# Recurrent layer of a two-layer encoder: input products by chunks through rotating PSUM banks, gates over two PSUM tiles, one exponential less, finished rows stored already split

## The chip, the cores and the metric

The kernel runs as one program on one core of a Trainium2 chip. The measured quantity is the device time of one execution in microseconds (us). The core has five engines that run their own instruction streams and wait for each other by semaphores: PE (TensorE, matrix products), DVE (VectorE), ACT (ScalarE), POOL (GpSimd) and SP (SyncE, which here issues every DMA). Matrix products land in PSUM, a memory of eight banks of 512 float32 columns by 128 partitions. Everything else lives in SBUF, or in DRAM between two stages.

## The reference, cut to what matters

The model has two layers over 1,040 tokens (16 meta tokens and 1,024 others) of width 1,024. The first is an attention layer, which the change does not touch. The second is recurrent:

```python
def odd_layer(z, w_in, conv_w, conv_b, w_a, b_a, w_x, b_x, lam, w_out):
    zp = z @ w_in                                  # (1040, 4096)
    u, gate = split_cols(zp, (2048, 2048))
    xc = conv_b + sum(pad(u)[tap:tap + T] * conv_w[tap] for tap in range(4))
    y = lru(xc, 0, reverse=False) + lru(xc, 1, reverse=True)
    return (y * silu(gate)) @ w_out

def lru(xc, d, reverse):                           # 16 blocks of 128 features
    r = sigmoid(xb @ w_a[d] + b_a[d]); i = sigmoid(xb @ w_x[d] + b_x[d])
    log_a = -8 * r * softplus(-lam[d])
    a = exp(log_a)
    b = sqrt(-expm1(2 * log_a)) * i * xc
    h_t = a_t * h_(t-1) + b_t                      # along the tokens
```

## The kernel before

**Number format.** Each matrix product is made of three products of a high and a low part, `hi` and `lo`, that are multiplied as float32r. Splitting a row means one rounding copy and one subtraction. Weights come by DMA into `wr` (256 KB each) and are split on POOL: line 106 writes `wh`, line 107 subtracts and writes `wl` (`wown` for the gates' weights). The weight rings have three `wr` and four `wh`/`wl` buffers.

**Blocks.** Features stand on the partitions, tokens along the rows. The recurrent layer goes through 16 blocks `e` of 128 features. For each block PE makes `pu`, the input product of `u` (three chunks of 348, 346 and 346 columns over eight contraction tiles, 72 matrix instructions), and `pg`, that of the gate (two chunks of 512, 48 instructions). Each is made in two halves of the contraction: in `half`, all chunks of the first four tiles stand ahead of all chunks of the other four. DVE scales `pu` into `ou` (line 1148). ACT and DVE make the convolution `oxc` (lines 1151 to 1154), which is split into `oxh` (ACT, line 757) and `oxl` (DVE, line 758). The silu of the gate is `og`, `otg` (lines 1140 to 1143).

**Two blocks behind.** While block e's input products run, PE also makes the four gate products `pz` of block e-1 (two directions, `r` and `i`), whose sigmoids are written as tanh (line 1180). For each direction ACT makes `oa` = a (line 1187), `osq` = a squared by a second exponential (line 1190) and a third tanh into `tz` (line 1191). DVE forms (osq + 1) * tz (line 1192) and (z + 1) * xc (line 1193). The rest of the recurrence belongs to block e-2 and is emitted after block e's convolution: one square root over both directions (ACT, line 1200, with a table load ahead of it and another behind it), a product (line 1203) and a scan (lines 1205 and 1207) per direction on DVE, the sum of the directions on POOL (line 1210), the product with the silu on DVE (line 1211), and a store of the finished row to DRAM (line 1212).

**Order.** A scheduler works out each engine's instruction order beforehand from the order in which the kernel emits work; weight loads and splits are emitted with a priority 200 steps ahead. On the chip each engine then takes its instructions in that order.

**PSUM.** One buffer of three banks for `pu`, a `big` tile of three banks for the gate products of both directions, and a `two` tile of two banks for `pg`.

**End.** The output product `oo` has eight tiles of 128 output features with 96 matrix instructions each, four quarters `qd` of the contraction of four finished rows each. The rows come back from DRAM in `y_load` (`oy`) and are split there: the first four while blocks 12 to 15 run (on POOL and DVE), the other twelve after block 15 (on ACT and DVE).

Of the kernel before, what the change touches and what calls it, by code (L numbers as in the profile page):

```python
# [16 lines left out]
P = 128  # L17
T = 1040
# [23 lines left out]
def trunk_kernel(ctx: ExitStack, tc: tile.TileContext, a: dict, out: bass.AP):  # L42
# [51 lines left out]
    def split_w(src, shape, nm, own=None, eng=nc.gpsimd):  # L94
# [4 lines left out]
        if own:  # L99
            hi, lo = [sb["P"].tile([P, 512], F32R, tag=own + z, name="wown", bufs=1) for z in "hl"]  # L100
# [48 lines left out]
    def parts(nm):  # L149
        """A row of T columns over three banks: (bank, first column, last column)."""  # L150
# [18 lines left out]
    def stat(sq, s, m, dst, tag=None, rt="S"):  # L169
        """Sums over features of the squares in sq, one row per selector column; the matrix part is put off."""  # L170
# [66 lines left out]
    s_y = [dram.tile([P, 1024], F32, name=f"s_y{i}") for i in range(16)]  # L237

# [188 lines left out]
    def fold(r, j, t0, t1):  # L427
        """Squares of a head's 128 features as two rows of 64, the pair's second head below the first."""
# [52 lines left out]
    def mla_scales():  # L481
        # score scales of the latent attention, by token, and the key norms, by row
# [45 lines left out]
    def steps(g, res):  # L528
        """Pass on the times that g yields; its tile goes to res."""
# [119 lines left out]
    class Unit:  # L649
        """One block of queries of two heads in the windowed attention."""  # L650
# [239 lines left out]
    def parts_c(nm, third="t"):  # L890
        """A row of T columns in the banks of the latent attention."""
# [169 lines left out]
    out_mm(ps0[0], 0, 0, 1)  # L1061
    ph.close()
    ph = phase(None, H=16, T=4, rs=1)
# [27 lines left out]
    psum({"b": 1, "big": 1, "two": 1})  # L1091

# [4 lines left out]
    # decay constants: c1 = -(8 / 2) * softplus(-lambda), half biases  # L1097
# [22 lines left out]
    c2n = const.tile([P, 32], F32, name="c2n")  # L1120
    nc.vector.tensor_scalar(c2n, pl_, -8.0, None, ALU.mult)
    c1p = const.tile([P, 32], F32, name="c1p")
    nc.vector.tensor_scalar(c1p, pl_, 4.0, None, ALU.mult)
# [4 lines left out]
    def w_gates(e):  # L1128
        return split_w(a["wg"][e], (4, P), "wg", "gw" if e < 15 else None)
# [4 lines left out]
    def half(e, isu, hf, ps):  # L1134
        wh, wl = split_w(a["w2"][2 * e + isu, hf], (4, P), "w2")
        mm3p(ps, [(wh[:, k], wl[:, k], h1h[4 * hf + k], h1l[4 * hf + k]) for k in range(4)], hf == 0, hf == 1)

    def gate_in(e, pg):
        g = row("og", "T")
        nc.vector.scalar_tensor_tensor(g[:, :1024], pg, 0.5, R["rs2"][:, NM:T], ALU.mult, ALU.mult)  # L1140
        tg = row("otg", "T")
        nc.scalar.activation(tg[:, :1024], g[:, :1024], AF.Tanh)
        nc.vector.scalar_tensor_tensor(tg[:, :1024], tg[:, :1024], 1.0, g[:, :1024], ALU.add, ALU.mult)
        return tg

    def conv(e, pu):
        u = row("ou", "X")
        evac(pu, lambda t, c: nc.vector.tensor_mul(u[:, c], t, R["rs2"][:, c]))
        xc = row("oxc", "X")
        cw = [vcol(V_CW + 4 * e + t) for t in range(4)]  # L1150
        nc.scalar.activation(xc, u, AF.Identity, scale=cw[2], bias=vcol(V_CB + e))
        nc.vector.scalar_tensor_tensor(xc[:, 2:T], u[:, 0:T - 2], cw[0], xc[:, 2:T], ALU.mult, ALU.add)
        nc.vector.scalar_tensor_tensor(xc[:, 1:T], u[:, 0:T - 1], cw[1], xc[:, 1:T], ALU.mult, ALU.add)  # L1153
        nc.vector.scalar_tensor_tensor(xc[:, 0:T - 1], u[:, 1:T], cw[3], xc[:, 0:T - 1], ALU.mult, ALU.add)
        return xc

    class Lru:
        """The recurrence of one block of features, in both directions."""

        def __init__(self, e, tg, xc, ch_, cl_):  # L1160
            self.e, self.tg, self.xc, self.c = e, tg, xc, (ch_, cl_)
            self.z = {}
# [4 lines left out]
        def gate(self, d, j, ps=None):  # L1167
            gh, gl = self.w
            e = self.e
            if ps is None:  # L1170
                ps = big("pz")
            n = T if d == 0 else T - NM
            ch, off = (CH, OFF) if d == 0 else (CHR, -NM)
# [4 lines left out]
            src = ps[:, OFF:OFF + T] if d == 0 else ps[:, :n]  # L1178
            bc = hb[:, 32 * j + 16 * d + e:32 * j + 16 * d + e + 1]
            nc.scalar.activation(z[:, :n], src, AF.Tanh, scale=0.5, bias=bc)  # L1180
            self.z[d, j] = z
# [14 lines left out]
        def scan(self):  # L1196
            tz = self.tz
            if True:
                nc.vector.memset(tz[:, 1, 1024:T], 0.0)
# [212 lines left out]
```

## Time and profile before

| what | value |
|---|---|
| median of 3 runs | 1963.94 us (1963.55 to 1967.7) |
| span of the profiled execution | 1963.5 us; no other time is shown for this execution, and the lowest of the three runs is 1963.55 us |
| granted TensorE clock, mean | 0.980 |
| busy: PE, DVE, ACT, POOL | 94%, 65%, 44%, 46% |
| recurrent layer, from its first product to the last instruction | 1241.6 to 1963.5 us |

PE, DVE, ACT and POOL are as above; PEld is PE's weight load and SPq the DMA queue of SP. In a timeline row stand the start and the duration in us, the engine, the line of the kernel, the operation and its output and input tiles, and in brackets the idle time before it and what ended it. In a row of a group the three numbers after the count are the shortest, the median and the longest duration in ns. In a row of the windows the engines' busy times in us are followed by the granted clock, the busy share of the DMA engines and the rate in GB/s. In a row of the chain stand start and length in us.

### The profile page before, as it was taken

The numbers are of one execution on the slowest core, as the hardware profiler recorded it, in microseconds if no ns is written. First come the engines' busy times: TensorE is split into PE (matmuls) and PEld (weight loads), VectorE is DVE, ScalarE is ACT, GpSimd is POOL, SyncE is SP. The second block draws the span as 40 slices with busy tenths as digits, with TensorE's granted clock in tenths as the row PEclk, the third lists the DMA queues.
The fourth block names the chain that finished last, engine by engine and source line by source line (L and its number), as shares of the span: only waits on it lengthen the run. The fifth ranks groups of instructions, "written<-read, shape, count | busy, mean of one in ns | idle before, by whom it ended". The sixth has DMA issues, their size and how long they took to land.

```text
span 1963.5 us, 28463 instructions
## 1 busy us (share of the span) xinstructions
PE 1837.2 (94%) x10822; PEld 1666.7 (85%) x10822; DVE 1272.3 (65%) x1953; ACT 859.7 (44%) x1394; POOL 908.1 (46%) x769
## 2 busy tenths in 40 slices
PE   8999989889999999998999999998989898889899
PEld 7987988889999999887888899887778787777687
DVE  7785368787663424889888743467878787887200
ACT  5355234454332202665666531156565656556000
POOL 5454455444225732434333333455656565654431
PEclk9999999999999999999999999999999998989899
DMA  5356422223223452322221023311111122124421
GB/s 177 82 171 248 116 77 69 63 69 85 81 64 128 152 174 90 87 88 67 66 75 52 23 87 131 92 53 54 59 54 60 54 68 67 65 79 147 171 81 43
DMA packets 107606, 180.19 MB, mean 92 GB/s; under 512 B 31759, under 2 KB 51343, under 8 KB 107470
## 3 DMA queue, kind: packets, MB, share of 16 engines
q1 hardware_dynamic: 107470, 178.37, 29.0%
q8 instruction: 85, 1.39, 0.3%
q14 instruction: 51, 0.42, 0.1%
HBM read 123.57 MB, written 46.77 MB: 87 GB/s over the span
## 4 chain that ended last, share of the span: by engine, by line
PE 50%; DVE 24%; ACT 8%; POOL 7%; issue 6%; DMA 3%; SPq 0%; POOLq 0%; DVEq 0%; ACTq 0%
PE pj L159 10%; PE oo L159 7%; PE pxop L159 6%; PE px L917 4%; PE av L997 4%; PE op L159 3%; PE up L159 3%; PE tp L981 3%; POOL osq L1210 3%; PE vps L425 2%; DVE osq L1207 2%; DVE oz L1203 2%; DVE oxc L1153 2%; DVE osq L1205 2%; DVE tz L1192 2%
## 5 line engine op out<-in xcount | busy, mean ns | idle before, releaser
L106 POOL TENSOR_SCALAR wh<-wr 128x512 fp32r<-128x512 f32 (+2 forms) x219 | 178.1, 813 | 522.5 <-PE pu L159 132.4
L107 POOL TENSOR_TENSOR wl<-wr,wh 128x512 fp32r<-128x512 f32 (+2 forms) x219 | 350.8, 1602 | 17.5
L159 PE MATMUL pj<-xh,wl 128*128 128x346 f32 (+1 forms) x768 | 252.0, 329 | 12.3 <-DVE wl L107 6.9
L159 PE MATMUL pj<-xl,wh 128*128 128x346 f32 (+1 forms) x768 | 249.6, 325 | 0.3 <-DVE xl L259 0.3
L159 PE MATMUL pj<-xh,wh 128*128 128x346 f32 (+1 forms) x768 | 249.0, 324 | 0.0
L159 PEld LDWEIGHTS pj<-xh,wl 128*128 128x128 f32 x768 | 146.7, 191 | 14.2 <-ACT xh L258 6.8
L159 PEld LDWEIGHTS pj<-xl,wh 128*128 128x128 f32 x768 | 146.9, 191 | 1.8 <-DVE xl L259 1.7
L159 PEld LDWEIGHTS pj<-xh,wh 128*128 128x128 f32 x768 | 146.8, 191 | 0.1
L159 PE MATMUL pu<-h1h,wl 128*128 128x346 f32 (+1 forms) x384 | 126.8, 330 | 0.8 <-issue 0.8
L159 PE MATMUL pu<-h1l,wh 128*128 128x346 f32 (+1 forms) x384 | 126.0, 328 | 0.0
L159 PE MATMUL pu<-h1h,wh 128*128 128x346 f32 (+1 forms) x384 | 125.8, 328 | 0.0
L119 PE MATMUL pz<-oxh,wown 128*128 128x512 f32 (+2 forms) x300 | 83.4, 379 | 45.1 <-ACT oz L1180 29.4
L935 POOL TENSOR_SCALAR mpm<-p,mmx 128x96 f32<-128x96 f32 (+1 forms) x69 | 25.6, 371 | 216.0 <-DVE mmx L930 123.3
L987 ACT CAST pth<-tp 128x512 fp32r<-128x512 f32 (+1 forms) x160 | 78.8, 507 | 82.9 <-PE tp L981 81.5
L988 DVE TENSOR_TENSOR ptl<-tp,pth 128x512 fp32r<-128x512 f32 (+1 forms) x160 | 92.0, 584 | 23.6 <-ACT pth L987 21.9
L159 PE MATMUL oo<-oyh,wl 128*128 128x512 f32 x256 | 102.1, 399 | 5.4 <-ACT oyh L1225 5.4
L159 PE MATMUL oo<-oyl,wh 128*128 128x512 f32 x256 | 102.2, 399 | 3.2 <-DVE oyl L1228 3.2
L159 PE MATMUL oo<-oyh,wh 128*128 128x512 f32 x256 | 102.1, 399 | 0.0
L119 PEld LDWEIGHTS pz<-oxh,wown 128*128 128x128 f32 x300 | 52.3, 204 | 58.6 <-issue 27.0
L159 PE MATMUL pg<-h1h,wl 128*128 128x512 f32 x256 | 101.7, 397 | 0.0
L159 PE MATMUL pg<-h1h,wh 128*128 128x512 f32 x256 | 101.5, 397 | 0.0
L159 PE MATMUL pg<-h1l,wh 128*128 128x512 f32 x256 | 101.3, 396 | 0.0
(448 smaller groups left out, 5562.9 us busy)
## 6 DMA issues: line engine op xcount, KB each, us to landing
wr<-in_w SPq DMA_DIRECT2D x128, 256.0 KB
wr<-in_wo SPq DMA_DIRECT2D x64, 256.0 KB
s_y<-osq SPq DMA_DIRECT2D x16, 512.0 KB
oy<-s_y SPq DMA_DIRECT2D x16, 512.0 KB
s_g<-gth SPq DMA_DIRECT2D x10, 520.0 KB
xr<-in_x SPq DMA_DIRECT2D x8, 520.0 KB
s_qn<-qr SPq DMA_DIRECT2D x8, 520.0 KB
s_kn<-kr SPq DMA_DIRECT2D x8, 520.0 KB
```

The source lines that it names most:

```text
L106: eng.tensor_scalar(hi[:, :n], raw[:, :n], 1.0, 1.0, ALU.mult, ALU.mult)
L107: eng.tensor_sub(lo[:, :n], raw[:, :n], hi[:, :n].bitcast(F32))
L119: nc.tensor.matmul(ps[:m, off + c0:off + c1], w, x[:, c0:c1], start=first and j == 0 and pi == 0, stop=last and j == nt - 1 and pi == 2)
L159: nc.tensor.matmul(t[:, :c1 - c0], w, x[:, c0:c1], start=first and j == 0 and pi == 0, stop=last and j == nt - 1 and pi == 2)
L425: nc.tensor.matmul(ps[:m, :n], s, w, start=j == 0 and pi == 0, stop=j == nt - 1 and pi == 2)
L917: nc.tensor.matmul(dst[:m, d0:d0 + a1 - a0], l[:, s], r[:, a0:a1], start=pi == 0, stop=pi == 4)
L981: nc.tensor.transpose(tp[:, o:o + m], p_[:m, NM + P * (kt + j):NM + P * (kt + j) + P], ident[:m, :m])
L987: nc.scalar.copy(hi[:, :w], tp[:, :w])
L988: nc.vector.tensor_sub(lo[:, :w], tp[:, :w], hi[:, :w].bitcast(F32))
L997: nc.tensor.matmul(av[:, :n], l[:, vs], pts[kt][o][:, j * n:j * n + n], start=kt == 0 and j == 0 and pi == 0, stop=False)
L1153: nc.vector.scalar_tensor_tensor(xc[:, 1:T], u[:, 0:T - 1], cw[1], xc[:, 1:T], ALU.mult, ALU.add)
L1210: nc.gpsimd.tensor_add(yv[:, :1024], self.z[0][2][:, NM:T], yv[:, :1024])
```

## The change

Only the recurrent layer changes. Blocks, arithmetic and output are the same, but for the following.

- PSUM is cut otherwise: a ring `c` of three single banks takes the chunks of `pu` and `pg` in turn, `big` takes the forward gates, `two` the backward gates.
- A chunk is finished over the whole contraction before the next begins, both weight halves being loaded first. Gate products stand between the chunks.
- The second exponential and `osq` are gone. The factor 1 - a*a is made from a tanh with half the scale, and the factor (a + 1) is applied on DVE after the root. The scan writes over its input.
- `root` (the square root) moves from the next block's scan to the end of its own block's gates. The formation of (a + 1) * root moves into `scan`.
- The finished row is split at once: ACT copies it (`oyh`), POOL subtracts (`oyl`, for blocks below 15), and both parts are stored: two stores of 512 KB for each of blocks 0 to 13. Blocks 14 and 15 stay in SBUF. `y_load` has no arithmetic left: two loads of 512 KB per row, the first of them after block 15's input products, since they take the place of the layer's input rows.
- The gates' own weights have two buffers instead of one, and the row of inverse norms has a fixed place.

The core of the diff:

```diff
-    psum({"b": 1, "big": 1, "two": 1})
+    psum({"c": 3, "big": 1, "two": 1})
...
+    def chunk_mm(w, halfs, t, c0, c1):
+        for hf in halfs:
+            wh, wl = w[hf]
+            for k in range(4):
+                x, xl_ = h1h[4 * hf + k], h1l[4 * hf + k]
+                for pi, (l, r) in enumerate(((wl[:, k], x), (wh[:, k], xl_), (wh[:, k], x))):
+                    nc.tensor.matmul(t[:, :c1 - c0], l, r[:, c0:c1], start=hf == 0 and k == 0 and pi == 0,
+                                     stop=hf == 1 and k == 3 and pi == 2)
...
-                nc.scalar.activation(sq[:, :n], tz[:, :n], AF.Exp, scale=c2, bias=c2)
-                nc.scalar.activation(tz[:, :n], tz[:, :n], AF.Tanh, scale=cp, bias=cp)
-                nc.vector.scalar_tensor_tensor(tz[:, :n], sq[:, :n], 1.0, tz[:, :n], ALU.add, ALU.mult)
...
+        def decay(self, d):
...
+            nc.scalar.activation(av[:, :n], tz[:, d, :n], AF.Exp, scale=cn, bias=cn)
+            nc.scalar.activation(tz[:, d, :n], tz[:, d, :n], AF.Tanh, scale=cp, bias=cp)
+        def root(self):
+            tz = self.tz
+            nc.vector.memset(tz[:, 1, 1024:T], 0.0)
+            nc.scalar.activation(tz, tz, AF.Sqrt, scale=0.25)
...
         def scan(self):
...
+                nc.vector.scalar_tensor_tensor(tz[:, d, :n], av[:, :n], 1.0, tz[:, d, :n], ALU.add, ALU.mult)
                 nc.vector.tensor_mul(ti[:, :n], ti[:, :n], tz[:, d, :n])
...
-            nc.sync.dma_start(s_y[self.e], yv[:, :1024])
+            nc.scalar.copy(yh_[:, :1024], yv[:, :1024])
+            (nc.gpsimd if e < 15 else nc.vector).tensor_sub(yl_[:, :1024], yv[:, :1024], yh_[:, :1024].bitcast(F32))
+            if e < 14:
+                nc.sync.dma_start(s_y[e], yh_[:, :1024].bitcast(F32))
+                nc.sync.dma_start(s_yl[e], yl_[:, :1024].bitcast(F32))
+            else:
+                yh[e], yl[e] = yh_, yl_
...
+            cur.u_chunk(0, w)
             prev.gate(0, 0)
+            cur.u_chunk(1, w)
+            prev.gate(1, 0)
+            prev.decay(0)
+            cur.u_chunk(2, w)
+        w = w2_load(e, 0)
+        cur.conv()
         if late:
             late.scan()
         if prev:
             prev.gate(0, 1)
+            prev.decay(1)
...
+                cur.g_chunk(0, w)
+                prev.gate(1, 1)
+                cur.g_chunk(1, w)
...
+            prev.root()
+        cur.silu()
...
+    for e in range(4):
+        y_load(e, "H")
```

**Place 1: DVE over one block, before.** The names are as above; the first `oz<-oz,tz` is the product with the root, `osq<-oa,oz` the scans, `osq<-osq,otg` the finished row.

```order
L1203 TENSOR_TENSOR oz<-oz,tz 128x1040
L1148 TENSOR_TENSOR ou<-pu,rs_14121 128x346
L1205 SCALAR_TENSOR_TENSOR osq<-oa,oz 128x1040
L1148 TENSOR_TENSOR ou<-pu,rs_14121 128x346
L1203 TENSOR_TENSOR oz<-oz,tz 128x1024
L1207 SCALAR_TENSOR_TENSOR osq<-oa,oz 128x1024
L1152 SCALAR_TENSOR_TENSOR oxc<-ou,vec,oxc 128x1038
L1211 TENSOR_TENSOR osq<-osq,otg 128x1024
L1153 SCALAR_TENSOR_TENSOR oxc<-ou,vec,oxc 128x1039
```

Now, from the first instruction behind the root to the convolution:

```order
L1239 SCALAR_TENSOR_TENSOR tz<-oa,tz 128x1040
L1239 SCALAR_TENSOR_TENSOR tz<-oa,tz 128x1024
L1159 TENSOR_TENSOR ou<-pu,rstd 128x348
L1195 SCALAR_TENSOR_TENSOR otg<-otg,og 128x1024
L1240 TENSOR_TENSOR oz<-oz,tz 128x1040
L1240 TENSOR_TENSOR oz<-oz,tz 128x1024
L1242 SCALAR_TENSOR_TENSOR oz<-oa,oz 128x1040
L1159 TENSOR_TENSOR ou<-pu,rstd 128x346
L1244 SCALAR_TENSOR_TENSOR oz<-oa,oz 128x1024
L1232 MEMSET tz 128x16
L1248 TENSOR_TENSOR oz<-oz,otg 128x1024
L1159 TENSOR_TENSOR ou<-pu,rstd 128x346
```

The last chunk of `ou`, which stood between the two scans, now stands behind the product of the finished row (line 1248, which waits for POOL's sum), and with it the whole convolution (lines 1165 to 1168) and `oxl`. The two (a + 1) * root instructions now stand between the root and the products.

**Place 2: ACT over the second part of a block, before**, from the split of the convolution to the root:

```order
L757 CAST oxh<-oxc 128x1040
L1142 ACTIVATE otg<-og 128x1024
L1180 ACTIVATE oz<-pz,hb 128x1024
L1187 ACTIVATE oa<-tz,c1n 128x1024
L1190 ACTIVATE osq<-tz,c2n 128x1024
L1191 ACTIVATE tz<-tz,c1p 128x1024
L1200 ACT_TABLE_LOAD
L1200 ACTIVATE tz<-tz 128x2080
```

Now:

```order
L1165 ACTIVATE oxc<-ou,vec 128x1040
L758 CAST oxh<-oxc 128x1040
L1250 CAST oyh<-oz 128x1024
L1215 ACTIVATE oz<-pz,hb 128x1040
L1227 ACTIVATE oa<-tz,c1n 128x1024
L1215 ACTIVATE oz<-pz,hb 128x1024
L1228 ACTIVATE tz<-tz,c1p 128x1024
L1233 ACT_TABLE_LOAD
L1233 ACTIVATE tz<-tz 128x2080
L1194 ACT_TABLE_LOAD
L1194 ACTIVATE otg<-og 128x1024
```

The silu's tanh moved behind the root, the second exponential left, and the copy of the finished row and the tanh of the other gate (`oz`, 1,040 columns) moved in between the split of the convolution and the root.

**Place 3: SP's DMA queue after block 15's input products, now.** `s_y_173` and `s_yl_187` are the two parts of finished row 0, the following numbers the following rows; `wr<-in_wo` are weights of the output product.

```order
L1264 DMA oyh<-s_y_173 128x1024
L1265 DMA oyl<-s_yl_187 128x1024
L1253 DMA s_y_186<-oyh 128x1024
L1254 DMA s_yl_200<-oyl 128x1024
L105 DMA wr<-in_wo 128x512
L1264 DMA oyh<-s_y_174 128x1024
L1265 DMA oyl<-s_yl_188 128x1024
L1264 DMA oyh<-s_y_175 128x1024
L1265 DMA oyl<-s_yl_189 128x1024
L1264 DMA oyh<-s_y_176 128x1024
L1265 DMA oyl<-s_yl_190 128x1024
```

The loads of rows 1 and up stand behind the two stores of row 13 (`s_y_186`, `s_yl_200`); behind row 4's loads follow two more weight loads and then rows 5 to 7.

More of the change, by code (lines that the diff above doesn't have):

```diff
@@ L99, in split_w @@
         if own:
-            hi, lo = [sb["P"].tile([P, 512], F32R, tag=own + z, name="wown", bufs=1) for z in "hl"]
+            hi, lo = [sb["P"].tile([P, 512], F32R, tag=own + z, name="wown", bufs=own_bufs) for z in "hl"]
         else:
@@ L1138, in gate_in @@
[L1138 to L1155, printed above, removed]
```

196 lines of the change are left out of this document (114 added, 82 removed).

## The prediction

> **What bounds the kernel now.** I read the page first, then the windows over the recurrent layer, the chain of waits, and the timelines of DVE, ACT and POOL over one block.
>
> ```profile
> span 1963.5 us, 28463 instructions
> PE 1837.2 (94%) x10822; PEld 1666.7 (85%) x10822; DVE 1272.3 (65%) x1953; ACT 859.7 (44%) x1394; POOL 908.1 (46%) x769
> ```
>
> By the page PE is full. The windows (length, then busy PE, PEld, DVE, ACT, POOL) tell another story of this layer:
>
> ```profile
> 1404.50:1437.00 32.50, 29.03 (x143) 25.71 (x144) 26.44 (x20) 19.29 (x17) 19.55 (x11) 0.95 0.17 57
> 1667.00:1703.00 36.00, 31.03 (x157) 27.66 (x156) 28.62 (x21) 18.99 (x17) 21.66 (x12) 0.91 0.20 66
> 1830.00:1963.50 133.50, 128.47 (x543) 103.42 (x542) 11.24 (x17) 0.00 (x0) 36.38 (x38) 0.97 0.28 92
> ```
>
> A block ("round" from here) takes 32.5 us, and 36 where rows are loaded back beside it; PE idles in each. Undisturbed PE runs, from the chain:
>
> ```profile
> 1303.03 3.83 PE pu L159 x24
> 1255.03 11.20 PE pg L159 x48
> ```
>
> Three chunks of 3.83 and 11.20 for `pg` make 22.7; the four gate products, some 3,120 columns three times over, add 1.4 each at `pg`'s rate. PE needs 28.3 us of the 32.5. What else sets the round? Its timeline, from one square root to the next:
>
> ```profile
> 1436.03 1.24 DVE L1203 TENSOR_TENSOR oz<-oz,tz 128x1040 f32<-128x1040 f32 x1 [1.00 <-ACT tz L1200]
> 1437.62 2.32 DVE L1205 TENSOR_TENSOR_SCAN osq<-oa,oz 128x1040 f32<-128x1040 f32 x1
> 1439.85 0.49 DVE L1148 TENSOR_TENSOR ou<-pu,rs 128x346 f32<-128x346 f32 x1
> 1440.43 1.26 ACT L1151 ACTIVATE oxc<-ou,vec 128x1040 f32<-128x1040 f32 x1 [1.99 <-POOL wh L106]
> 1441.51 3.27 DVE L1207 TENSOR_TENSOR_SCAN osq<-oa,oz 128x1024 f32<-128x1024 f32 x1
> 1444.70 1.27 DVE L1152 SCALAR_TENSOR_TENSOR oxc<-ou,vec,oxc 128x1038 f32<-128x1038 f32 x1
> 1444.92 3.31 POOL L1210 TENSOR_TENSOR osq<-osq 128x1024 f32<-128x1024 f32 x1 [2.29 <-DVE osq L1207]
> 1448.27 1.62 DVE L1211 TENSOR_TENSOR osq<-osq,otg 128x1024 f32<-128x1024 f32 x1 [2.30 <-POOL osq L1210]
> 1449.81 2.33 DVE L1153 SCALAR_TENSOR_TENSOR oxc<-ou,vec,oxc 128x1039 f32<-128x1039 f32 x1
> 1454.90 1.06 ACT L757 CAST oxh<-oxc 128x1040 fp32r<-128x1040 f32 x1 [6.57 <-DVE oxc L1154]
> 1460.82 1.10 ACT L1180 ACTIVATE oz<-pz,hb 128x1024 f32<-128x1024 f32 x1
> 1461.81 1.23 ACT L1187 ACTIVATE oa<-tz,c1n 128x1024 f32<-128x1024 f32 x1
> 1464.21 1.24 ACT L1191 ACTIVATE tz<-tz,c1p 128x1024 f32<-128x1024 f32 x1
> 1465.47 1.28 ACT L1200 ACT_TABLE_LOAD   x1
> 1466.77 1.94 ACT L1200 ACTIVATE tz<-tz 128x2080 f32<-128x2080 f32 x1
> ```
>
> The root that ends at 1436.0 releases DVE, DVE releases POOL's sum, the sum releases DVE again, DVE releases ACT, and ACT ends the next root at 1468.7. **The round is a ring through DVE, POOL and ACT**, and PE waits for it. Over the layer, from the first root to the one before block 15:
>
> ```profile
> 1302.72 1.95 ACT L1200 ACTIVATE tz<-tz 128x2080 f32<-128x2080 f32 x1
> 1735.93 1.94 ACT L1200 ACTIVATE tz<-tz 128x2080 f32<-128x2080 f32 x1
> ```
>
> Thirteen rounds take 1737.87 - 1304.67 = 433.2 us, 33.3 each. The time before is 1,304.7 + 433.2 + 225.6 behind that root.
>
> **A second limit inside the ring.** DVE instructions with two SBUF inputs, and POOL's, come in two lengths:
>
> ```profile
> L1193 DVE SCALAR_TENSOR_TENSOR oz<-oz,oxc x32: 1211/1228/2327, 1283.6 to 1796.6; 128x1040 f32<-128x1040 f32 x16, 128x1024 f32<-128x1024 f32 x16
> L1210 POOL TENSOR_TENSOR osq<-osq x16: 3232/3312/3336, 1314.6 to 1814.5; 128x1024 f32<-128x1024 f32 x16
> 1448.90 2.15 POOL L107 TENSOR_TENSOR wl<-wr,wh 128x512 fp32r<-128x512 f32 x1
> 1459.98 0.62 POOL L106 TENSOR_SCALAR wh<-wr 128x512 fp32r<-128x512 f32 x1
> 1460.68 1.26 POOL L107 TENSOR_TENSOR wl<-wr,wh 128x512 fp32r<-128x512 f32 x1
> ```
>
> The `wl` of 1448.90 stands under the finished-row product (to 1449.89) and ends at 1451.05, 1.16 behind it; the convolution step of 1449.81 ends 1.1 after that. The two engines take turns, whole instructions at a time: a split of 0.62 + 1.26 that falls on a busy stretch of DVE lengthens it by its own length. The `ou` rows, with one input in PSUM, keep 0.5.
>
> **The change part by part: the ring.** I walk the new orders from the end of a root, start to start.
> 1. DVE, eight instructions and a scan pair as place 1 shows them: two (a + 1) * root at 1.15, `ou` 0.43, silu 1.15, two products at 1.15, scan 2.23, `ou` 0.43, scan 2.26 (3.27 less the 1.0 that it waited for the split before it): 11.1. Removing `osq` takes an instruction from ACT, but its DVE partner is only moved, from a place beside ACT's work to this stretch: +2.3.
> 2. POOL's sum. Before, the convolution step that started at 1444.70 held it up until 1445.97; it ended 2.26 later. Now nothing of DVE with two inputs stands beside it: 2.3, ending at 13.5. At the upper bound it is 3.3 as in every row of it.
> 3. The finished row's product 1.6 (the next `wh` slips in ahead, as at 1448.27), then the last `ou` 0.5, which no longer stands ahead of the sum: 15.6. ACT's `oxc` 1.35: 16.95. Before, `oxc` and the first convolution step were hidden beside scan and sum; now they are on the ring.
> 4. Three convolution steps, each reading the one before, at the shortest of this row, 1.29, and one `wl` of the next splits, 1.2, since two splits follow the sum on POOL: 22.0.
>
> ```profile
> L1154 DVE SCALAR_TENSOR_TENSOR oxc<-ou,vec,oxc x16: 1289/1642/1693, 1271.8 to 1755.4; 128x1039 f32<-128x1039 f32 x16
> ```
>
> 5. ACT, as place 2 shows: split 0.96, copy of the finished row 0.95, tanh 1.0, exponential 1.14, tanh 1.0, tanh 1.26, table load 1.30, root 1.94: 9.6, ending at 31.5. The exponential saves 1.15; the copy and the other tanh, which had their place in ACT's idle 6.57 us, cost 1.95. PE's gate products are long done by then.
>
> So **31.5 if POOL meets DVE nowhere else**. It does. POOL's order is now: sum, two splits, subtraction of the finished row, three splits. The subtraction cannot start before ACT's copy at 24.0; with `oxl` and the two (z + 1) * xc taking turns, subtraction (2.3, as the sum) and two splits end 0.9 after the new root: +0.9 on step 1. The raw gates' weights can be fetched only then (third `wr` buffer), and a fetch takes
>
> ```profile
> 1237.24 2.69 DMA wr<-in_wg
> ```
>
> so their split falls into the middle of step 1, +1.65 of its 1.9. **Round: 31.5 + 0.9 + 1.65 = 34.05 us**, bounds 31.5 (no meeting) and 35.1 (sum at 3.3). Thirteen: 442.7, which is **+9.4** on 433.2. The nine or so plain rounds lose 1.5 each; the four with 36 gain 2, since the work of `y_load` is gone from them.
>
> By the Trainium skill, page "SBUF — State Buffer", section "Who interferes with whom", a DVE instruction with two SBUF inputs and a POOL instruction that reads SBUF exclude each other for a whole instruction; so 1.05 of the sum's 3.31 was waiting, and the trace's turn-taking agrees. By the row alone, 3.3 in all 16 cases, the round would be 35.1 and the thirteen +23.
>
> **At nothing**, with what hides it: the ring of three banks (a chunk needs the bank of the third before it, whose `ou` or `og` DVE has read some 6 us earlier; PE has 5.7 us a round to give, and with less cover it would give those first); PE's slower clock behind a gap of 5 us (the same slack); the second store of a round (DMA share 0.17 of the windows becomes some 0.2; its hold on SP is in the 1.65 above); the gates' second weight buffer; the one table load pair, which stays a pair.
>
> **The start.** Of block 0 all 72 products now stand ahead of the norm's products, not 36:
>
> ```profile
> 1249.31 5.73 PE pu L159 x36
> 1263.76 1.37 DVE L1148 TENSOR_TENSOR ou<-pu,rs 128x348 f32<-128x348 f32 x3 [4.82 <-DMA rs<-d_rstd]
> ```
>
> The row of norms comes 5 later, at 1268.7. The gate's second chunk waits for DVE to read the first of the same tile, to 1270.8, and PE idles some 10 us. From there the rest of `pg` and `pu` and two gate products reach block 1's last `pu` chunk at 1289.9, some 1.7 later at the lower clock after such a gap (an estimate from windows like the 0.91 above). Then `ou`, `oxc`, convolution, split, two tanh, exponential, tanh, load and root as in steps 3 to 5, without the copy: 15.8. The first root ends at 1307.4 instead of 1304.7: **+2.7** (bounds 0 and 5, the whole delay).
>
> **The end.** Before, the finished row 15 was late:
>
> ```profile
> 1820.99 3.58 DMA s_y<-osq
> 1824.62 3.65 DMA oy<-s_y
> 1830.70 128.24 PE oo L159 x542
> 1825.00:1832.00 7.00, 2.10 (x4) 1.40 (x5) 1.27 (x2) 1.04 (x1) 1.26 (x1) 0.55 0.88 319
> ```
>
> Store, load and split of row 15 are gone: if all else is ready, up to 15 us (PE's idle time between 1756 and 1831: 74.5 less 225 products at 0.236 and 5.7 of gates). But place 3: loads of rows 1 to 3 wait on SP behind the store of row 13, whose low part is ready only 28 us behind the root before block 15; rows 5 to 7 wait behind two weight loads, whose buffers come free when POOL splits two weights behind the sum of row 14, at 48 us. At 3.6 us for the first transfer and 1.65 to 1.9 for each following one (0.52 MB at the 319 GB/s above, or somewhat less) row 3 is there at 43, row 7 at 62. ACT's tanh of block 15's last gates, which frees the PSUM of output tiles 1 and 2, stands behind a root and two table loads, at 50. At 80 PE has done 144 of the 768 products, at 89 168. The remaining 600 at 0.2366 (128.24 / 542) and the last 4.6 make 89 + 142 + 4.6 = 235, less 1 of slack: 234 instead of 225.6, **+8.3** (bounds -8, dense from block 15's gates on, and +14).
>
> **Sum**: 1963.5 + 9.4 + 2.7 + 8.3 = **1984 us**. The page's span and the lowest run (1963.55) differ by less than 0.1, the median is 0.4 above; I leave it out.
>
> **Rivals.**
> 1. *Clashes fall away* (20%). If POOL's splits settle into ACT's part of the ring and into the sum's wait, the round is 31.5 to 32.3. For it: POOL is free for some 12 of 32 us, and ACT's 9.6 has DVE nearly idle. Against: the subtraction now fills that stretch first. Thirteen rounds of 31.8: 413, or -20; with start and end 1955. Slower turns into faster below a round of 32.5.
> 2. *The end is dense* (12%): rows arrive in time and nothing waits for row 15. Then -8 at the end: 1963.5 + 9.4 + 2.7 - 8 = 1968.
> 3. *PE becomes the bound* (6%): the change does what its chunks are for, the ring closes below 28.3, and PE sets the round at some 29: 13 x (29 - 33.3) = -56, some 1915. Steps 1 to 5 would have to be 2.5 us shorter than their bare sum; no row says so.
> 4. *More clashes* (12%): sum at 3.3, and the second convolution step blocked as at 1449.81 once more: 35.5 a round, 2003.
>
> **How the numbers follow.** The forecast's case has 50%, with its own range 1973 to 1996 (round 33.3 to 34.8). About 0.2%, 4 us, is what a measurement of this kernel can tell from no change. Slower: the forecast, rival 4 and half of rival 2, 68%. Faster: most of rival 1, and rival 3, 20%. The range leaves out rival 3 and the far end of rival 4: 1952 to 1999.
>
> **What would show it.** The roots' distance in the timeline (34 against 32), the idle time of DVE ahead of the finished row's product (2.4), the last `ou` of a block directly behind it, ACT's idle time ahead of `oxh`, long (a + 1) * root rows, PE idle some 5 us a block ahead of `pz`. At the end: SP's wait ahead of the loads of rows 1 and 5. The forecast is wrong if the sum is not followed by the last `ou`, if roots stand 32 apart, or if PE has no gap between 20 and 50 us behind the root before block 15.

## The result: 0.8% slower, and the profile after

The changed kernel takes 1979.05 us (median of 4 runs, 1977.17 to 1983.98) against 1963.74 us (1961.56 to 1967.7): a ratio of 1.0078, 95% interval 1.006 to 1.0096. The forecast was 1984. The profiled execution has a span of 1975.3 us, 11.8 above the one of before (1963.5); the sums below explain this difference.

First the page, then the windows over one round, to be read against those of before (32.50 us with PE busy 29.03 at a clock of 0.95):

```profile
span 1975.3 us, 28456 instructions
PE 1841.0 (93%) x10822; PEld 1669.4 (85%) x10822; DVE 1250.1 (63%) x1953; ACT 823.9 (42%) x1367; POOL 903.7 (46%) x780
```

```profile
1434.00:1467.60 33.60, 29.08 (x144) 25.03 (x143) 26.64 (x21) 17.64 (x16) 19.94 (x13) 0.95 0.21 71
```

PE still idles, 4.5 us in these windows. The timeline from one root to the next, with the instructions that close the ring:

```profile
1434.81 1.95 ACT L1233 ACTIVATE tz<-tz 128x2080 f32<-128x2080 f32 x1
1436.78 2.99 DVE L1239 SCALAR_TENSOR_TENSOR tz<-oa,tz 128x1040 f32<-128x1040 f32 x2 [1.77 <-ACT tz L1233]
1440.16 1.65 POOL L106 TENSOR_SCALAR wown<-wr 128x512 fp32r<-128x512 f32 x1 [2.63 <-DMA wr<-in_wg]
1441.26 3.88 DVE L1240 TENSOR_TENSOR oz<-oz,tz 128x1040 f32<-128x1040 f32 x2
1447.70 2.28 DVE L1244 TENSOR_TENSOR_SCAN oz<-oa,oz 128x1024 f32<-128x1024 f32 x1
1450.05 2.41 POOL L1247 TENSOR_TENSOR oz<-oz 128x1024 f32<-128x1024 f32 x1 [6.00 <-DVE tz L1232]
1452.49 1.62 DVE L1248 TENSOR_TENSOR oz<-oz,otg 128x1024 f32<-128x1024 f32 x1 [2.50 <-POOL oz L1247]
1454.04 0.50 DVE L1159 TENSOR_TENSOR ou<-pu,rstd 128x346 f32<-128x346 f32 x1
1454.58 1.26 ACT L1165 ACTIVATE oxc<-ou,vec 128x1040 f32<-128x1040 f32 x1 [10.78 <-DVE ou L1159]
1460.82 1.06 ACT L758 CAST oxh<-oxc 128x1040 fp32r<-128x1040 f32 x1 [4.99 <-DVE oxc L1168]
1461.79 1.04 ACT L1250 CAST oyh<-oz 128x1024 fp32r<-128x1024 f32 x1
1462.90 2.51 POOL L1251 TENSOR_TENSOR oyl<-oz,oyh 128x1024 fp32r<-128x1024 f32 x1 [4.61 <-ACT oyh L1250]
1468.42 1.95 ACT L1233 ACTIVATE tz<-tz 128x2080 f32<-128x2080 f32 x1
```

Roots stand 33.6 us apart (33.65 in the mean of the thirteen rounds). DVE waits 2.50 for the sum, the last `ou` stands directly behind the finished row's product, ACT waits 10.78 for that `ou`, and the split of the gates' weights (`wown`), whose fetch came 2.63 late, stands between the products and makes them 3.88 instead of 2.3. The chain of waits shows a second way around the same ring: from the sum through two splits to POOL's wait for ACT's copy `oyh`, the subtraction, three splits, the fetch and `wown`.

At the end, PE's idle rows behind the last root of the rounds (which ends at 1739.53), and the clock in two windows:

```profile
1765.28 1.21 PE L119 MATMUL pz<-oxh,wl 128*128 128x272 f32 x3 [5.82 <-ACT oz L1215]
1774.90 1.22 PE L159 MATMUL oo<-oyh,wl 128*128 128x512 f32 x2 [3.40 <-DMA oyh<-s_y]
1793.96 0.77 PE L159 MATMUL oo<-oyh,wl 128*128 128x512 f32 x1 [6.69 <-ACT oz L1215]
1797.28 1.22 PE L159 MATMUL oo<-oyh,wl 128*128 128x512 f32 x2 [2.56 <-DMA oyh<-s_y]
```

```profile
1775.00:1780.00 5.00, 4.86 (x11) 3.44 (x12) 5.00 (x4) 5.00 (x6) 0.00 (x0) 0.50 0.99 367
1795.00:1800.00 5.00, 2.72 (x6) 2.15 (x7) 5.00 (x4) 0.00 (x0) 1.33 (x1) 0.50 0.99 342
```

Four waits, 18.5 us, and behind the longer of them PE runs at half its clock for 5 us and more.

| part | before | after | difference | forecast |
|---|---|---|---|---|
| up to the end of the first root | 1304.67 | 1302.14 | -2.5 | +2.7 |
| thirteen rounds | 433.2 | 437.4 | +4.2 | +9.4 |
| behind the root before block 15 | 225.6 | 235.8 | +10.2 | +8.3 |

The first row holds 1.9 us that is hardly the change's: the first product of the layer starts at 1239.71 in this execution and at 1241.6 in that of before, and in the traces of the kernels below, whose edits all lie behind it, anywhere from 1238.18 to 1246.63.

### The profile page after: what moved, and what is told of

It reads as the page before. It is cut to its first block, busy times and chain, and to the rows that moved or that the text cites. A ratio compares the mean times of both kernels' runs of the same rounds, so it can differ in the third digit from the quotient of the medians.

```text
span 1975.3 us, 28456 instructions
## 1 busy us (share of the span) xinstructions
PE 1841.0 (93%) x10822; PEld 1669.4 (85%) x10822; DVE 1250.1 (63%) x1953; ACT 823.9 (42%) x1367; POOL 903.7 (46%) x780
## 4 chain that ended last, share of the span: by engine, by line
PE 51%; POOL 18%; issue 12%; DVE 11%; DMA 5%; ACT 2%; SPq 0%; POOLq 0%; DVEq 0%; ACTq 0%
PE pj L159 10%; PE oo L159 9%; POOL wl L107 7%; PE pxop L159 5%; PE px L918 4%; PE av L998 4%; POOL wh L106 3%; PE tp L982 3%; PE up L159 3%; PE op L159 3%; PE vps L426 2%; POOL oyl L1251 2%; POOL oz L1247 2%; DMA wr<-in_wg 2%; PE py L918 2%
## 5 line engine op out<-in xcount | busy, mean ns | idle before, releaser
L106 POOL TENSOR_SCALAR wh<-wr 128x512 fp32r<-128x512 f32 (+2 forms) x219 | 171.6, 784 | 393.9 <-PE pj L159 95.3
L107 POOL TENSOR_TENSOR wl<-wr,wh 128x512 fp32r<-128x512 f32 (+2 forms) x219 | 336.6, 1537 | 17.4
L119 PE MATMUL pz<-oxh,wown 128*128 128x272 f32 (+1 forms) x300 | 83.5, 380 | 36.7 <-ACT oz L1215 36.7
L1275 DVE TENSOR_TENSOR hres<-oo,hres 128x512 f32<-128x512 f32 x16 | 10.6, 689 | 149.5 <-PE oo L159 149.5
```

Source lines behind the costliest of these rows:

```text
L106: eng.tensor_scalar(hi[:, :n], raw[:, :n], 1.0, 1.0, ALU.mult, ALU.mult)
L107: eng.tensor_sub(lo[:, :n], raw[:, :n], hi[:, :n].bitcast(F32))
L119: nc.tensor.matmul(ps[:m, off + c0:off + c1], w, x[:, c0:c1], start=first and j == 0 and pi == 0, stop=last and j == nt - 1 and pi == 2)
```

## Experiments

All kernels start from the changed one. Several runs differ by a few us in what happens ahead of the layer, so rounds are read as the distance of roots in the trace, and the end as the time behind the fourteenth root (237.7 us in the changed kernel: 1737.58 to 1975.3).

**The subtraction on DVE.**

```diff
-            (nc.gpsimd if e < 15 else nc.vector).tensor_sub(yl_[:, :1024], yv[:, :1024], yh_[:, :1024].bitcast(F32))
+            nc.vector.tensor_sub(yl_[:, :1024], yv[:, :1024], yh_[:, :1024].bitcast(F32))
```

> The subtraction that splits a finished row (oyl) is done on DVE for every block instead of on POOL. Ring theory (the forecast's): POOL's chain loses 2.5 us a round, the two meetings with the new root's DVE work (0.9 and 1.65) fall away, DVE gets 1.2 at a place beside ACT's work: round 31.5 to 32.3 instead of 33.65, 1951 to 1962 us. Port theory (rival: DVE instructions with two SBUF inputs and POOL's instructions together fill the round, 19.1 + 14.4 = 33.5 of 33.65 by the rows of the changed kernel): -2.5 + 1.2 = -1.3 a round, 1962 us. PE theory (rival: input products and the PSUM ring set the round): nothing, 1979 us.

Measured: 1972.14 us, 1.0036 of before (1.0023 to 1.0049). Roots stand 33.2 apart ((1702.06 - 1303.31) / 12), not 31.5 to 32.3, and not the 32.35 of the port theory either. DVE, POOL and SP in one round of it:

```profile
1471.42 3.85 DVE L1239 SCALAR_TENSOR_TENSOR tz<-oa,tz 128x1040 f32<-128x1040 f32 x2 [1.14 <-ACT tz L1233]
1463.57 2.15 POOL L107 TENSOR_TENSOR wl<-wr,wh 128x512 fp32r<-128x512 f32 x1
1466.83 0.33 SPq L1254 DMA_DIRECT2D s_yl<-oyl  x1
1467.26 0.37 SPq L105 DMA_DIRECT2D wr<-in_w  x1
1467.73 0.74 SPq L105 DMA_DIRECT2D wr<-in_wg  x1
```

POOL has no subtraction any more and is through with its four splits at 1465.7, but the gates' weights are fetched only at 1467.73, and their split still meets the first instructions behind the root: the pair takes 3.85 (2.99 in the changed kernel), while the two products now take 2.36 instead of 3.88. So the meeting with `wown` hangs on the late fetch, and not on POOL's load alone. What makes the fetch late here is another thing than in the changed kernel; see the last run.

**The rounding copies on ACT**, in the 16 blocks only.

```diff
-            eng.tensor_scalar(hi[:, :n], raw[:, :n], 1.0, 1.0, ALU.mult, ALU.mult)
+            nc.scalar.copy(hi[:, :n], raw[:, :n])
```

> In the 16 blocks the rounding copy of each weight (wh, 0.62 us on POOL, five a round) is made by ACT; POOL keeps the subtraction (wl). Ring theory: POOL's meetings fall away, but ACT gets one copy of 0.6 between the last tanh and the root: round 32.1, 1959 us. Port theory: 5 x 0.62 = 3.1 us less of a full port: round 30.4 to 30.6, 1937 to 1940 us. PE theory: nothing, 1979 us. If ACT's copies have to wait for their weights, the round gets longer: 35 and more, over 1990 us.

Measured: 1985.96 us, 1.0101 (1.0081 to 1.0122); roots 34.0 apart. A row of DVE, and the windows over a round:

```profile
1444.43 3.42 DVE L1245 TENSOR_TENSOR_SCAN oz<-oa,oz 128x1040 f32<-128x1040 f32 x1
```

```profile
1436.30:1470.30 34.00, 29.90 (x152) 26.48 (x151) 26.12 (x20) 20.23 (x21) 14.00 (x7) 0.95 0.22 70
```

POOL's busy time falls from 19.9 to 14.0 a round, and the round gets longer. That refutes the port theory for this kernel (30.4 to 30.6): the round is not the sum of what DVE and POOL do. The ring theory's 32.1 was missed as well, since POOL's meetings did not fall away. What counts is what stands on the ring: the copy of 0.61 ahead of the root (at 1467.27), and `wl` and `wown`, which still meet the pair behind the root and now the first scan (3.42 instead of 2.3).

**The second exponential back.**

```diff
+            nc.scalar.activation(sq[:, :n], tz[:, d, :n], AF.Exp, scale=c2, bias=c2)
             nc.scalar.activation(tz[:, d, :n], tz[:, d, :n], AF.Tanh, scale=cp, bias=cp)
+            nc.vector.scalar_tensor_tensor(tz[:, d, :n], sq[:, :n], 1.0, tz[:, d, :n], ALU.add, ALU.mult)
...
-                nc.vector.scalar_tensor_tensor(tz[:, d, :n], av[:, :n], 1.0, tz[:, d, :n], ALU.add, ALU.mult)
```

> One part of the change undone: the second exponential and osq are back, (osq + 1) * tz is formed behind the gates again and the two (a + 1) * root behind the root are gone; all else stays. Ring theory: DVE loses 2.3 at the head of the ring, gets 1.2 ahead of the last ou (one of the two stands there now) and ACT gets 1.15 ahead of the root: 0, 1979 us (1975 to 1983). Port theory: the same DVE work at another place: 0. Rival (ACT sets the round, and the exponential less was a gain): +1.15 to +2.3 a round, 1994 to 2009 us. Rival (DVE's stretch behind the root sets it alone): -2.3 a round, 1949 us.

Measured: 1979.46 us, 1.0072 (1.0047 to 1.0096), the changed kernel's time; roots 33.8 apart. Inside this ring "one exponential less" is worth nothing: what ACT saves ahead of the root, DVE pays behind it. (In this kernel the root waits 1.46 us for DVE's second (osq + 1) * tz.)

**Rows stored whole.** The copy, the subtraction and the second store of rows 0 to 13 are undone; these rows are split by ACT and DVE behind their loads.

```diff
+            if e < 14:
+                nc.sync.dma_start(s_y[e], yv[:, :1024])
+                return
```

> One part of the change undone: rows 0 to 13 are stored whole and split behind their loads by ACT and DVE, as the kernel before did; the round loses ACT's copy, POOL's subtraction and a store. To be read: the distance of the roots. Ring theory: the copy (1.0) leaves the ring, and the subtraction's meetings are gone, round 32.0 to 32.6 instead of 33.65. Rival (what the split costs a round is nothing, since ACT and POOL are idle half the time): 33.6.

Measured, in one execution and so without an interval: 1945.33 us; roots 30.6 apart from the third round on, less than expected (32.7 and 32.1 in the first two). The end is no longer for it: 1943.6 - 1706.31 = 237.3. DVE's pair behind the root and the windows:

```profile
1463.44 2.38 DVE L1239 SCALAR_TENSOR_TENSOR tz<-oa,tz 128x1040 f32<-128x1040 f32 x2 [1.34 <-ACT tz L1233]
1458.69 0.33 SPq L105 DMA_DIRECT2D wr<-in_wg  x1
```

```profile
1430.00:1460.60 30.60, 28.96 (x151) 25.30 (x152) 24.49 (x21) 16.74 (x15) 16.50 (x11) 1.00 0.18 61
```

**This is where the loss was.** Splitting each finished row at once costs 3.05 us in a settled round and 35.9 us over the thirteen (437.4 against 401.5); the rest of the change is a gain, since 1945 is below the kernel before. Of that rest only the exponential was run alone, and it is worth nothing; which part gains stays open. Of the 3.05, ACT's copy is 1.0. The fetch of the gates' weights now goes out 2.8 us ahead of the root's start (1458.69 against 1461.45) instead of 2.8 behind it, and its split meets nothing there: the pair takes 2.38 and the two products 1.24 and 1.20, together 2.05 less than in the rows of the changed kernel.

**The finished row behind the convolution.** `issue_after(x)` queues an instruction behind x on the same engine, without a wait. First only the product (line 1248) moves, behind the third convolution step; then also ACT's copy, behind the root:

```diff
+        def finish(self, dve=None, act=None):
+            with tc.issue_after(dve.ins):
                 nc.vector.tensor_mul(yv[:, :1024], yv[:, :1024], self.tg[:, :1024])
+            with tc.issue_after(act.ins):
                 nc.scalar.copy(yh_[:, :1024], yv[:, :1024])
...
             prev.root()
+            late.finish(cur.last, prev.rt)
```

> As in the run with the finished row behind convolution and root, but only the product is moved behind the third convolution step; its copy stays ahead of the root on ACT. Ring theory: sum (2.4) and product (1.6) leave the ring, but the copy now waits for the product behind the convolution, 0.2 and 1.0: round 33.65 - 4.0 + 0.2 = 29.9, with one meeting more 31; 1931 to 1945 us. POOL's subtraction stands ahead of two splits and waits for the copy: if POOL's chain sets the round, 32 to 33, 1958 to 1971 us.

Measured: 1950.72 us, 0.9922 (0.9897 to 0.9948); roots 31.4 apart, 0.4 more than the upper figure of the ring theory and 0.6 less than the lower one of POOL's chain: neither case.

> Only the order is changed: the finished row's product (line 1248) is issued on DVE behind the third convolution step, and its copy on ACT (oyh) behind the root; the sum on POOL stays where it is. Ring theory: POOL's sum (2.4), the product (1.6), and the copy (1.0) leave the ring, which is then 31.6 - 5.0 = 26.6 plus one to two meetings of 1.1, below what PE needs (28.3): PE becomes the bound, round 28.5 to 29.5 instead of 33.65, thirteen rounds 54 to 67 less, 1912 to 1925 us. Rival (the new PSUM ring or PE's order sets the round): nothing, 1979 us. Rival (POOL's chain sets it: its subtraction now waits for the root and holds the splits of the gates' weights behind it, sum, four splits 7.6, wait for the root, subtraction 2.5, fetch 2.6, split 1.9): 32 to 34 a round, 1958 to 1984 us.

Measured: 1946.57 us, 0.9898 (0.9877 to 0.992); roots 31.2 apart. An order alone, no instruction more or less, takes 2.4 us out of a round and beats the kernel before. But PE did not become the bound. Windows and a stretch of DVE and POOL behind the convolution:

```profile
1424.00:1455.20 31.20, 28.79 (x152) 25.29 (x151) 29.22 (x21) 17.65 (x16) 23.26 (x13) 1.00 0.24 76
```

```profile
1447.68 1.61 POOL L106 TENSOR_SCALAR wh<-wr 128x512 fp32r<-128x512 f32 x1
1448.73 1.63 DVE L1253 TENSOR_TENSOR oz<-oz,otg 128x1024 f32<-128x1024 f32 x1
1449.38 2.12 POOL L107 TENSOR_TENSOR wl<-wr,wh 128x512 fp32r<-128x512 f32 x1
1450.29 2.31 DVE L759 TENSOR_TENSOR oxl<-oxc,oxh 128x1040 fp32r<-128x1040 f32 x1
1457.55 5.18 DVE L1240 SCALAR_TENSOR_TENSOR tz<-oa,tz 128x1040 f32<-128x1040 f32 x2 [0.55 <-ACT tz L1234]
1458.53 3.11 POOL L1257 TENSOR_TENSOR oyl<-oz,oyh 128x1024 fp32r<-128x1024 f32 x1 [0.25 <-ACT oyh L1256]
```

DVE's pause at the sum is gone, and with it a stretch in which POOL met nobody. Now the two engines alternate, one instruction each, for most of the round: DVE is busy 29.2 of 31.2, each step lengthened by POOL's in between, and the subtraction, now behind the root, makes the pair 5.18. That these turns set the 31.2 is read from the rows; the kernels under "All together" test it. By the Trainium skill, page "SBUF — State Buffer", section "Who interferes with whom", a DVE instruction with two SBUF inputs contends with a POOL instruction that reads SBUF; this trace agrees, with 1.24 against 2.31 for `oxl` and 1.29 against 2.12 for `wl`.

**The end: earlier loads, then the last gates first.** Row 13 stays in SBUF, and the loads of rows 0 to 7 are emitted together ahead of block 15's gates. The second kernel also issues ACT's copy of row 14 behind the tanh of block 15's last gates (the last line of the diff).

```diff
-            if e < 14:
+            if e < 13:
...
-    for e in range(4):
+    for e in range(8):
         y_load(e, "H")
...
     prev.gate(1, 1)
+    late.finish(None, prev.zt)
```

> Only the end is changed: row 13 is kept in SBUF (no stores, no loads of it), and the loads of rows 0 to 7 are all issued before block 15's gates. Order theory (the forecast's): rows 1 to 7 no longer wait on SP behind row 13's stores and two weight loads; of PE's idle rows the 3.4 and 2.6 us that ended with oyh<-s_y fall away, the rounds stay at 33.65: 5 to 9 us less, 1970 to 1974 us. Rival (the idle time of the end is ACT's tanh of the last gates, 5.8 and 6.7 us, and the rest only moves there): 0 to 2 us less, 1977 to 1979 us. Rival (DMA bytes are the limit of the end): 4 of 28 row loads and 2 stores fewer, about 0.52 MB at 300 GB/s = 1.7 us each, all of it gained: 10 us less.

Measured: 1979.65 us, 1.0074 (1.0055 to 1.0093): nothing. (The expectation's third case should have said two loads and two stores fewer.) PE's waits over the layer's end by releaser:

```profile
PE pz L119 <- ACT oz L1215: 5.8, 1, 5.8
PE oo L159 <- DMA oyl<-s_yl: 4.6, 5, 3.0
PE oo L159 <- ACT oz L1215: 4.0, 1, 4.0
PE oo L159 <- DMA oyh<-s_y: 1.4, 3, 0.5
```

The waits for rows 0 to 7 became shorter, and new ones stand behind 150 products, at rows 8 to 11. 15.8 us remain of 18.5; the end is 0.6 shorter.

> The end with row 13 kept and loads 0 to 7 early, as in the run of the end, and ACT's copy of row 14 issued behind the tanh of block 15's last gates instead of ahead of them (with that, no second pair of table loads between). Order theory: of the changed kernel's idle PE rows 6.7 (ACT oz) falls to 0 to 1, and tiles 1 and 2 start some 5 to 10 us earlier: 4 to 7 us less than with the loads alone, 1972 to 1976 us. Rival (PE's idle time only moves to the next wait, the loads, as it did when only the loads were moved): 1978 to 1980 us.

Measured: 1976.27 us, 1.0055 (1.0034 to 1.0075). The end takes 233.6 instead of 237.7 (the fourteenth root starts at 1741.34). The two edits together give back 4.1 of the 10.2 that the end lost, 0.6 of it by the loads alone: behind the earlier loads ACT's order counted for more than SP's. ACT's order without them was not run, and a new wait of 3.4 for POOL's `wl` took the place of the one for ACT.

**All together.** Three kernels with the finished row's product behind the convolution. The first two have the second kernel's end; the third stores its rows whole and has of that end only row 14's copy behind the last gates.

> The finished row behind convolution and root, the rounding copies wh of the 16 blocks on ACT (5 x 0.6 a round), and the end with row 13 kept, loads 0 to 7 early and row 14's copy behind the last gates. Port theory for the round of 31.2 that was left (DVE and POOL now wait for each other nearly without a gap: what they hold each other up, some 1.08 for each of 12 DVE instructions with two SBUF inputs, 2.2 for each scan, 2.2 for sum and subtraction, 0.53 and 1.1 for the parts of a split, makes 29.9): 5 x 0.53 = 2.6 less, and PE's 28.3 or the ring (26.6 plus 0.6) bounds: round 28.5 to 29.5, 1946.6 less 22 to 35, less 3 for the end: 1909 to 1922 us. Ring theory without the port (the 31.2 is latency): ACT's copies ahead of the root lengthen it: 31.8 to 32.4, 1951 to 1959 us. Rival (PE or its PSUM ring is the 31.2): nothing but the end, 1943 us.

Measured: 1952.08 us, 0.9925 (0.9911 to 0.994), roots 32.0 apart: longer, as the ring theory without the port had it (31.8 to 32.4, 1951 to 1959 us), where the port theory had 28.5 to 29.5. One round of it:

```profile
1503.08 0.62 ACT L107 CAST wown<-wr 128x512 fp32r<-128x512 f32 x1 [1.58 <-DMA wr<-in_wg]
1503.61 1.12 ACT L1219 ACTIVATE tz<-pz,hb 128x1040 f32<-128x1040 f32 x1
1504.78 0.74 PE L122 MATMUL pz<-oxh,wown 128*128 128x272 f32 x3 [2.76 <-ACT tz L1219]
```

ACT waits with a weight copy for the late fetch; behind it stands the tanh that frees the gates' PSUM, and PE waits 2.76 for that. The copies are cheap by duration and dear by their place.

> As the run before, and the subtraction oyl on DVE instead of on POOL (1.08 less of the shared time, but its instruction stands ahead of the products behind the root on DVE). Port theory: PE or the ring is the bound by now, the subtraction adds 1.2 to DVE's stretch behind the root: the same round or up to 1 longer, 1909 to 1935 us. If the port were still the bound: 1.1 shorter a round, 14 us less than the run before.

Measured: 1944.31 us, 0.9885 (0.9868 to 0.9901), roots 31.7 apart. The subtraction on DVE is worth 0.3 a round here, where one case had 1.1 and the other no gain.

> Rows 0 to 13 stored whole as the kernel before did (no copy, no subtraction, one store a round), and the product of the finished row behind the convolution; wh stays on POOL; at the end row 14's copy behind the last gates. Port theory: 29.9 less 2.2 for the subtraction = 27.7, ring 26.6 with one meeting 27.7: PE's 28.3 bounds, round 28.5 to 29.5, against 30.6 with the product in its old place; thirteen rounds 14 to 27 less than the run with whole rows, 1918 to 1931 us. Ring theory without the port: the same. Rival (30.6 is PE's or PSUM's bound): 1942 to 1945 us.

Measured: **1909.85 us, 0.9714 (0.9698 to 0.9731)**, the fastest kernel here: 56 us below the kernel before on the same chip (1965.65) and 69 below the changed one. Roots are 28.6 apart. The time is 8 below the expected range, though the round lies within its own (28.5 to 29.5): the first root comes 4.5 earlier and the end is 3.7 shorter than with whole rows and the product in its old place. PE has no wait left in the rounds:

```profile
1488.00:1518.00 30.00, 30.00 (x159) 26.69 (x158) 27.23 (x23) 17.62 (x15) 21.16 (x12) 1.00 0.21 62
```

PE is busy 30.00 of 30.00: it is the bound, at 28.6 a round where the prediction read a need of 28.3. So 30.6 was no bound of PE or PSUM; the sum and the product still lay on the ring there. The run fits the turns of DVE and POOL as what set the 31.2, but it takes away ACT's copy and a store together with POOL's subtraction.

**Stores behind the fetch.** Last, an attempt to tell what holds the gates' weights back when the subtraction is on DVE; `ld` is the last fetch of the next gates' weights:

```diff
+            with tc.issue_after(ld.ins):
                 nc.sync.dma_start(s_y[e], self.y[0][:, :1024].bitcast(F32))
```

> The subtraction on DVE as in the run of that name, and in addition the two stores of a finished row are issued on SP behind the fetches of the next weights (of the gates, and two or three more) instead of ahead of them; DVE, ACT and POOL keep their order. To be read: the distance of the roots, 33.24 with the subtraction on DVE alone. Queue theory (the fetch of the gates' weights stands on SP behind the store of the low part, 1466.83, and goes out 1467.73; so their split meets the (a + 1) * root pair, 3.79 instead of 2.36): the fetch goes out some 2 to 4 us earlier, the pair is 2.4 to 2.6, round 31.7 to 32.1; thirteen rounds 15 to 20 less, 1952 to 1958 us. Rival (the fetch waits for a wr buffer and not for SP): 33.2, 1972 us.

Measured: 1970.4 us, 1.0029 (1.0017 to 1.0041); roots 33.2 apart, as without the edit. The run itself tells nothing: its order moved the stores behind an earlier fetch only, and in the trace the store of the low part (1467.11) still stands ahead of the fetch in question (1468.00), with one other fetch between.

The traces answer the question all the same. With the subtraction on DVE, SP waits with the store of the low part for `oyl`, 2.6 us on average (the row below, over thirteen rounds), and the fetch follows without a wait of its own, 2.0 us behind the end of POOL's last split (1463.57 + 2.15 = 1465.72), in eleven of the rounds. There SP's order holds it.

```profile
SPq L1254 <- DVE oyl L1251: 33.1, 13, 2.6
```

In the changed kernel the fetch goes out 0.02 us behind that split (1437.56 against 1437.54) and waits for the `wr` buffer, as the prediction said. What the round would be with the stores really behind the fetch is not shown.

## Why the prediction was right, and where its sizes were off

**What bounds the kernel: right.** The ring through DVE, POOL and ACT was the bound, and moving work off it moved the time. With sum and product moved off the ring and copy and subtraction gone the round fell to what PE needs. One of the forecast's signs was off in size: PE idles 3.0 us a block ahead of `pz` (33.3 in eleven), not some 5.

**The ring: 33.65 for 34.05.** By the steps of the prediction, from the rows after:

| step | forecast | measured |
|---|---|---|
| 1, DVE from the root to the end of the second scan, with both meetings | 13.65 | 13.2 (1436.78 to 1449.98) |
| 2, POOL's sum | 2.4 | 2.5 (to 1452.46) |
| 3, product, last `ou`, `oxc` | 3.45 | 3.4 (to 1455.84) |
| 4, convolution with one `wl` | 5.05 | 4.9 (to 1460.73) |
| 5, ACT to the end of the root | 9.6 | 9.6 (to 1470.37) |

The sum is 2.4 (16 rows, 2373 to 2429 ns), not the 3.3 of before. The meetings cost 2.2 instead of 2.55 (0.69 on the pair behind the root and 1.52 on the products), and they were the main term that was off; the convolution gives 0.15. A round is 0.4 shorter than forecast, over thirteen 5.2 us, all of the difference between +9.4 and +4.2. One remark of the prediction does not hold: of its thirteen rounds before, three and not four take 36 (35.8, 36.2, 35.8), and nine rounds of +1.5 with four of -2 make 5.5 and not 9.4. Its sum does not rest on that.

**The start: +2.7 forecast, -2.5 measured; this step failed in sign.** Of the -2.5, 1.9 is the earlier start of the layer, so the step itself gave -0.6. Its first half held: PE idles for the norms, 8.2 us for "some 10".

```profile
1266.15 0.63 PE L1143 MATMUL pu<-h1h,wl 128*128 128x348 f32 x1 [8.22 <-DVE ou L1298]
1266.00:1268.50 2.50, 2.35 (x7) 2.27 (x8) 1.78 (x4) 1.26 (x1) 0.00 (x0) 0.50 0.00 0
1288.13 1.26 ACT L1165 ACTIVATE oxc<-ou,vec 128x1040 f32<-128x1040 f32 x1 [3.28 <-DVE ou L1159]
```

What failed is the time at which PE goes on. It is 26.4 us behind the layer's first product, where the forecast had 29.2 (1270.8 - 1241.6): the row of norms came 1.3 earlier than "5 later", and the first product behind the gap is not the gate's second chunk, which the forecast waited for, but one of block 1's `pu`, which needs only the first `ou`. The slower clock behind the gap did show, 0.50 in the windows above (1.00 again from 1269 on), and the way from there to the last `pu` chunk took 21.4, near the 19.1 + 1.7 of the forecast. From `oxc` to the end of the root (1302.14) it took 14.0 and not 15.3: the first convolution met no split.

**The end: +10.2 for +8.3; near by two errors that nearly cancel.** The order on SP and ACT delayed it as forecast: rows 5 to 7 go out behind two weight loads, and ACT's last tanh came at 53 us instead of 50. But 80 us behind the root the trace has 118 products where the forecast had 144, and at 89 us 157 where it had 168. PE lost more than forecast ahead of 80 us, and between 80 and 89, where the forecast had 24 products, it ran without a gap and made 41. The clock was a part left out: behind gaps of 5.8, 3.4 and 6.7 us PE was busy for some 16 us at a clock of 0.50, by an estimate from that number 8 us lost; 26 products at 0.2366 are 6.2. No run shows the end without the slow clock. The Trainium skill states such a rule (page "TensorE: Matmul & The Clock Gate", section "Part 1: The HAM clock gate": half the clock after an idle window of about 3.4 us, full again after a busy one). These three gaps agree with it, but in the rounds a gap of 1.88 us was enough (last section), and there the measurement decides. The prediction put the clock into the start, and left it out of the end, where more hung on it.

**The rivals.** "Clashes fall away" did not come by itself; the runs show what it would take (an earlier fetch, no split of the rows): 30.6. "PE becomes the bound" was right as a possibility, "some 29" a round against 28.6 measured, but needed 5 us less on the ring, which the change does not take off. The forecast named the split's costs (copy 0.95, meetings 0.9 and 1.65, together 3.5); undoing it gave back 3.05.

## What to carry to other kernels

When no engine is full in a stage, follow one ring of waits around it and count what stands on it; work that is free by load (a copy on an engine that is 42% busy) costs its full length on the ring, and an order that takes it off can be worth more than removing instructions. Then look which pause you closed: here the engines that had taken turns unnoticed began to hold each other up, and only with the work gone, not moved, did PE become the bound. And where a cheap instruction waits for a late transfer, ask what is queued behind it.

## What was not expected of the hardware

- Scans are held up by POOL too: 2.3 us alone, 3.42 with POOL's `wown` beside them, the same 1.1 as for a product of two rows (the prediction had read the 3.27 of before in this way).
- When DVE and POOL both have work without a pause, they alternate, one instruction each, in the stretch shown; a 0.62 us copy on POOL then reads 1.61 and a 1.29 us subtraction 2.12 to 2.16. The longest victim was the pair behind the root, 5.18 for 2.3.
- Short gaps can halve PE's clock too. In the kernel before (and again behind 1.89 us at 1494.5, though not behind 2.01 at 1331.8):

```profile
1364.23 0.71 PE L119 MATMUL pz<-oxh,wown 128*128 128x272 f32 x3 [1.88 <-ACT oz L1180]
1365.00:1368.30 3.30, 3.30 (x13) 3.11 (x12) 2.22 (x2) 3.25 (x4) 0.49 (x1) 0.50 0.27 79
```

- In these kernels idle time in two pieces is no better than in one. PE's waits (1300 to 1700: total, count, longest) and the windows over thirteen rounds, first of the changed kernel, then of the one with the subtraction on DVE:

```profile
PE pz L119 <- ACT oz L1215: 33.3, 11, 3.4
1300.19:1737.58 437.39, 397.13 (x1999) 350.38 (x1998) 347.65 (x261) 229.90 (x195) 258.45 (x157) 0.96 0.21 71
```

```profile
PE pz L119 <- ACT oz L1215: 16.1, 11, 2.5
PE pu L1143 <- DVE og L1174: 16.0, 10, 2.0
1303.31:1735.22 431.91, 394.78 (x1994) 347.73 (x1993) 351.18 (x273) 229.85 (x195) 230.11 (x146) 0.96 0.21 72
```

Both idle about 3 us a round in these waits, one in a single piece of up to 3.4 us, the other in two pieces of up to 2.5 and 2.0; the mean clock is 0.96 in both. A single round can mislead here: that of the second kernel from 1436.23 to 1469.45 shows 1.00, ten of its other twelve 0.94 to 0.96.
